# A one-core decoder step: how the memory tokens' squares are summed, where a spreading product stands, and when the second key tiles are scaled

## The chip, the core and the metric

The kernel runs on one core of a Trainium2 chip. A core has TensorE (PE in the profile, its weight loads apart as PEld), VectorE (DVE), ScalarE (ACT), GpSimd (POOL) and SyncE (SP, which issues most transfers here). Each engine works through its own queue in order and waits where an operand, written by another engine, is not there yet. The metric is device microseconds of one launch, taken as the median of several runs.

## What is computed

One decoder layer serves 1024 prompt tokens and 8 x 4 sample tokens with the same weights: a mixer of gated groups (A) and latent attention (B), a cross-attention into 256 memory tokens, and a gated feed-forward part with a short convolution. Two pieces of the reference matter here. The keys and values of the memory tokens:

```python
def mem_kv(mem, g_mem_in, w_mk, w_mv, g_mk):
    n, m, _ = mem.shape
    hm = rms_norm(mem, g_mem_in)
    k = rms_norm((hm @ w_mk).reshape(n, m, MEM_HEADS, MEM_HEAD_DIM), g_mk)
    v = (hm @ w_mv).reshape(n, m, MEM_HEADS, MEM_HEAD_DIM)
    return k, v
```

And the latent attention's queries and keys, each normalised per head before the scores (the prompt has 8 heads and blocks of 128 tokens; the samples attend to 4096 cached tokens):

```python
q = (rms_norm(cq, g_q_a) @ w_uq).reshape(n, t, MLA_HEADS, QK_HEAD)
q = qk_rope(rms_norm(q, g_qk_q), pos)
...
k = qk_rope(rms_norm(jnp.concatenate([k_nope, k_pe], axis=-1), g_qk_k), pos)
...
p = jax.nn.softmax(s, axis=-1)
```

`rms_norm(x, g)` is x divided by the root of its mean square, times g.

## The kernel before

Every larger product is taken in three: both operands are split into a high part (a cast, mostly on ScalarE) and a low part (the rest, mostly on VectorE, lines 200 to 207), and high x high, high x low and low x high are accumulated (`mm3`, line 185). The stages follow one another: input projection, prompt attention (`phase2a`), the samples' attention over the cache pages (`phase2b`), the memory tokens (`mem_kv`), the output projection, cross-attention, feed-forward.

**Order.** Inside a `manual_schedule` block the engines it names keep the order in which the program writes their instructions. All others are ordered by the framework's planner, which runs the program in simulated time when it is built. `behind(a, b)` adds an order without a wait: a stands behind b in the queue.

**The prompt attention** keeps TensorE, ScalarE, VectorE and GpSimd in written order; SP is the planner's. It runs in steps t = 0, 1, 2, ... Each step transposes probabilities (L996), starts the scores of the next unit (`units[n]["a"]`, products on L185, maxima on VectorE in L979 and L983), multiplies values (L1011), and then runs the functions in `extra[t]`: projections for later heads, the steps of their normalisation, transpositions of keys and queries (L949), and `weight_sums`, which prepare sums of feed-forward weights on GpSimd (L839 to L842) through two buffers that SP loads and stores. `times` lists the steps at which the 26 weight sums stand.

Heads 0 to 3 have two groups of four key and query tiles (`proj_group`). The second group's normalisation is a generator, `norm`, of which a call runs the part up to the next `yield`. Its parts are: the sums of squares and the start of the inverse root (L903 to L905, L232 to L234), two Newton steps (L241 to L246), the query's factors and rotation (L911), and the scaling of the keys (two VectorE products in L925, one GpSimd product in L926). Two parts run ahead of step 0; the rest of them, scaling included, at step 0. The transpositions that need these keys stand at step 2, and between the two, at step 1, stand the maxima of the next unit's third and fourth score tiles.

**The memory tokens** come at the end of the samples' attention, where only SP keeps the written order and the planner orders the other four engines. `mem_kv` is a generator as well, so that its parts are emitted between those of the last sample batch. It multiplies the keys of four heads (L1545), squares the raw memory rows for the mean square per token (L1558, summed on GpSimd in L1560 into `acc`), multiplies the values in four groups of twelve products (`values(0)`, `(2)`, `(4)`, `(6)`), sums the squares over partitions with one-column products against ones (L1579, L1581), takes the inverse roots, and scales the keys with diagonal products (L1600, L1601).

Beside it the last sample batch ends its softmax (`batch_softmax`): inverse roots of the last keys on GpSimd (L248 to L255), scaling of the scores (L1423), maxima (L1426, L1452), a transposition on TensorE (L1455), a maximum (L1458) made into a diagonal (L1460), and the spreading product, which brings the maxima to all partitions:

```python
self.spread = nc.tensor.matmul(bc, self.ones[:32], s["dg"], start=True, stop=True)
```

Then come a copy (L1465), a subtraction (L1466), the exponential (L1468) and the products with the cached values (L1475, L1477). The first product of `values(6)` is put `behind` the spreading product. The output projection (products of `mx0`, `mx1`, `mx2` with `w_o`) follows; its second and third thirds of tokens are loaded by SP as `raw<-mix` into a ring of three buffers, which the weights of `mem_kv` use as well.

Of the kernel before, what the change touches and what calls it, by code (L numbers as in the profile page):

```python
# [5 lines left out]
F32 = mybir.dt.float32  # L6
FR = mybir.dt.float32r
I32 = mybir.dt.int32
AF = mybir.ActivationFunctionType
ALU = mybir.AluOpType  # L10
AX = mybir.AxisListType
PSUM = bass.MemoryType.PSUM

P = 128
# [140 lines left out]
class Net:  # L155
# [502 lines left out]
    def phase2a(self):  # L658
# [31 lines left out]
        norm = qk1[9:]  # L690
# [52 lines left out]
        spread(late[1][1], 25, 30)  # L743
        spread(late[2][0], 24, 30)
        sums = [(i, z) for i in (NK, NK + 1, *range(NK)) for z in range(2)]
        times = (1, 2, 3, 4, 5, 7, 8, 9, 11, 12, 14, 15, 16, 25, 26, 27, 29, 30, 36, 37, 39, 40, 41, 43, 44, 46)
        for t, x in zip(times, sums):
            extra[t].append(lambda x=x: self.weight_sums(half(), *x))

# [17 lines left out]
        with tc.manual_schedule(engines={E.PE, E.Activation, E.DVE, E.Pool}):  # L767
            for f in preps[0][0], preps[0][1], v1[0], preps[1][0], preps[1][1]:
                f()
            for e in range(4):  # L770
                units[0]["a"](e)
                if e:
                    units[0]["e"](e - 1)
                    if e % 2:
                        v1[e // 2 + 1]()
            units[0]["e"](3)
            for f in norm[:2]:
                f()
            extra[0][:0] = norm[2:]
            extra[1][:0] = v1[3:]  # L780
            steps, outs, pend, V = [], {}, [], []
            self.lows = []
            t = 0
            for n, u in enumerate(units):
                for k, banks in enumerate(u["steps"]):
                    self.flush()
                    for b in banks:
                        u["T"](b)
                    for f in outs.pop(t, []):
                        f()  # L790
                    for f in pend:
                        f()
                    pend = []
                    for w, e in jobs[t]:
                        w["a"](e)
                        pend.append(lambda w=w, e=e: w["e"](e))
                    self.flush()
                    for f in V:
                        f()
                    V = [lambda u=u, b=b: u["V"](b) for b in banks]  # L800
                    if k == len(u["steps"]) - 1:
                        outs.setdefault(t + 2, []).append(u["copy"])
                        outs.setdefault(t + 3, []).append(u["out"])
                        if order[n] == (7, 0):
                            outs[t + 3].append(lambda: steps.append(mix()))
                    for f in extra[t]:
                        f()
                    t += 1
                    if t == 32:
                        steps.append(sample())  # L810
                    steps = [x for x in steps if next(x, 0) is None]
            self.flush()
            self.lows = None
            for fs in [V] + [outs[t] for t in sorted(outs)] + [[]] * 4:
                for f in fs:
                    f()
                steps = [x for x in steps if next(x, 0) is None]
            assert not steps
# [48 lines left out]
    def proj_group(self, p, pp, hf, i0, i1, s, c, tt=("tp", 4)):  # L867

        nc = self.nc
        m, tn = i1 - i0, TILES[i0][1]  # L870
        r = kk = q = None

        def alloc():
            nonlocal r, kk, q
            r = self.t(p, [P, 4, 2, 4], F32, "hr", 2)[:tn, :m]
            kk = self.t(p, [P, 4, 4, 96], F32, "k", 2) if i0 < 8 else None
            q = self.t(p, [P, 4, 4, 96], F32, "q", 2) if i0 < 8 else self.qs[:, hf * 4 : hf * 4 + 4].unsqueeze(1)

        def part(i, z):
            t0, e = TILES[i][0], i - i0  # L880
            a, b = (self.cqh, self.cql) if z == 0 else (self.ckh, self.ckl)
            x = [(a[:, k, t0 : t0 + tn], b[:, k, t0 : t0 + tn]) for k in range(2)]
            w, n = ((s["wq"], 384), (s["wk"], 256), (s["wv"], 256))[z]
            ps = self.t(pp, [P, 512], F32, *tt)[:tn, :n]
            self.mm3(ps, x, w)
            if z == 2:
                nc.scalar.copy(s["v"][:, i], ps.rearrange("p (h d) -> p h d", h=4))
                return
            pv = ps.rearrange("p (h d) -> p h d", h=4)
            if z == 0 or i < 8:  # L890
                nc.scalar.copy(kk[:, e, :, :64] if z else q[:, e], pv)
            sq = self.t(p, [P, 4, n // 4], F32, f"hsq{z}", 2)[:tn]
            if z == 1 and (i >= 4 if hf else i < 6):
                for j in range(4):
                    nc.scalar.activation(sq[:, j], pv[:, j], AF.Square, accum_out=r[:, e, z, j : j + 1])
                return
            nc.scalar.activation(sq, pv, AF.Square)
            nc.vector.tensor_reduce(r[:, e, z], sq, AX.X, ALU.add)

        def norm():  # L900
            sc = self.sq_tok[:tn, i0:i1].unsqueeze(2).broadcast_to([tn, m, 4])
            rq, rk = r[:, :, 0], r[:, :, 1]
            nc.vector.tensor_tensor(rq, rq, sc, ALU.mult)  # L903
            nc.vector.tensor_tensor(rq, rq, sc, ALU.mult)
            nc.vector.tensor_tensor(rk, rk, c["kss"][:tn, i0:i1].unsqueeze(2).broadcast_to([tn, m, 4]), ALU.add)  # L905
            rf = r.rearrange("p m z h -> p (m z h)")
            yield from self.rsqrt_steps(p, rf, rf, 1.0 / 96)
            yield
            if i0 < 8:

                nc.vector.tensor_tensor(c["rq"][:, i0:i1, hf * 4 : hf * 4 + 4], rq, sc, ALU.mult)  # L911
            else:
                nc.vector.tensor_tensor(rq, rq, sc, ALU.mult)
                nc.vector.tensor_tensor(q, q, rq.unsqueeze(3).broadcast_to([tn, m, 4, 96]), ALU.mult)
            for e in range(0, m, 2):
                z = slice(e, min(e + 2, m))
                x = q[:, z, :, 64:]
                self.rope_tok(p, x, x, [t[:tn, i0 + z.start : i0 + z.stop] for t in c["qt"]], 4, tn, z.stop - e)
            if i0 == 8:
                nc.vector.tensor_copy(self.rn[:, hf * 4 : hf * 4 + 4], rk[:, 0])  # L920
                return
            yield
            for a, eng in ((slice(0, m // 2), nc.vector), (slice(m // 2, m), nc.gpsimd if hf else nc.vector)):
                x = kk[:, a, :, :64]
                eng.tensor_tensor(x, x, rk[:, a].unsqueeze(3).broadcast_to([P, m // 2, 4, 64]), ALU.mult)  # L925
            nc.gpsimd.tensor_tensor(  # L926
                kk[:, :, :, 64:], self.kr[:, i0:i1].unsqueeze(2).broadcast_to([P, m, 4, 32]),
                rk.unsqueeze(3).broadcast_to([P, m, 4, 32]), ALU.mult,
            )
            for e in range(m):  # L930
                s["q", i0 + e], s["k", i0 + e] = q[:, e], kk[:, e]

        qk = [lambda i=i, z=z: part(i, z) for i in range(i0, i1) for z in range(2)]
        it = norm()
        return [alloc] + qk + [lambda: next(it, 0)] * 6, [lambda i=i: part(i, 2) for i in range(i0, i1) if i < 8]

    def head_prep(self, p, pp, h, s, c):

# [580 lines left out]
    def mem_kv(self, raws, wk0):  # L1519
# [5 lines left out]
        self.t(pp, [P, 512], F32, "free", 1)  # L1525
        st = self.t(pp, [P, 512], F32, "st", 1)
        mh, ml = (self.t(p, [P, 8, 256], FR, x) for x in ("mh", "ml"))
        acc = self.t(p, [P, 256], F32, "acc")
        mr = [r.rearrange("p (k n) -> p k n", k=4) for r in raws[1:3]]
        xs = [(mh[:, k], ml[:, k]) for k in range(8)]  # L1530
        kr, sq = [], []
# [1 line left out]
        for h in range(4):  # L1533
# [18 lines left out]
            sq.append(self.t(p, [P, 256], F32, "sq", 4))  # L1552
            nc.scalar.activation(sq[h], ps, AF.Square)
            yield
        for k in range(8):
            x = mr[k // 4][:, k % 4]
            s2 = acc if k == 0 else self.t(p, [P, 256], F32, "msq", 2)
            nc.scalar.activation(s2, x, AF.Square)  # L1558
            if k:
                nc.gpsimd.tensor_tensor(acc, acc, s2, ALU.add)  # L1560
        yield
        av = [self.t(pp, [P, 512], F32, f"v{i}") for i in range(2)]

        def values(k):
            wh, wl = (x.rearrange("p k n -> p (k n)").rearrange("p (k n) -> p k n", k=2) for x in self.stream(I["w_mv"][k // 2], 8))
            for i in range(2):
                t = slice(i * P, i * P + P)
                x = self.mm3(av[i], [tuple(x[:, t] for x in xs[k + e]) for e in range(2)],
                             [(wh[:, e], wl[:, e]) for e in range(2)], first=k == 0, last=k == 6)
                if k == 6 and i == 0:  # L1570
                    self.behind(x, self.spread)

        values(0)
# [4 lines left out]
            for i in range(2):  # L1578
                nc.tensor.matmul(st[:, 2 * h + i : 2 * h + i + 1], sq[h][:, i * P : i * P + P], self.ones[:, :1], start=True, stop=True)  # L1579
        for i in range(2):  # L1580
            nc.tensor.matmul(st[:, 8 + i : 9 + i], acc[:, i * P : i * P + P], self.ones[:, :1], start=True, stop=True)  # L1581
        rt = self.t(p, [P, 2], F32, "rt")
        r2 = self.t(p, [P, 2], F32, "r2")
        r = self.t(p, [P, 4, 2], F32, "r")
# [870 lines left out]
```

## Time and profile before

| what | value |
|---|---|
| median of 3 runs | 1844.83 us (1842.12 to 1846.34) |
| the profiled execution | 1843.82 us, its span 1842.1 us |
| mean granted clock of TensorE | 0.994 of full speed |
| TensorE busy | 1809.4 us, 98% of the span |
| VectorE, ScalarE, GpSimd busy | 1354.1, 922.9, 697.1 us |
| moved by the transfers | 261.18 MB, 142 GB/s on the mean |

A timeline's line reads: start in us from the beginning of the span, duration in us, engine, line of the kernel, operation, what it writes `<-` what it reads, shape, `x` the number of instructions merged, and in brackets how long the engine stood idle before it and for whom. A group's line reads: line, engine, operation, count, minimum/median/maximum duration in ns, first and last start. A stretch's line reads: its bounds, its length, each engine's busy time (PE, PEld, DVE, ACT, POOL, with counts), TensorE's granted clock, and the transfers' share and rate.

### The profile page before, as it was taken

The numbers are of one execution on the slowest core, as the hardware profiler recorded it, in microseconds if no ns is written. First come the engines' busy times: TensorE is split into PE (matmuls) and PEld (weight loads), VectorE is DVE, ScalarE is ACT, GpSimd is POOL, SyncE is SP. The second block draws the span as 40 slices with busy tenths as digits, with TensorE's granted clock in tenths as the row PEclk, the third lists the DMA queues.
The fourth block names the chain that finished last, engine by engine and source line by source line (L and its number), as shares of the span: only waits on it lengthen the run. The fifth ranks groups of instructions, "written<-read, shape, count | busy, mean of one in ns | idle before, by whom it ended". The sixth has DMA issues, their size and how long they took to land.

```text
span 1842.1 us, 39314 instructions
## 1 busy us (share of the span) xinstructions
PE 1809.4 (98%) x14222; PEld 1706.1 (93%) x14222; DVE 1354.1 (74%) x2805; ACT 922.9 (50%) x1916; POOL 697.1 (38%) x852
## 2 busy tenths in 40 slices
PE   9999999999999999999999999999999999999999
PEld 8999777779999999998899979999999999999999
DVE  7855767757778776786645666898888888878664
ACT  7435667766555555555433556533333333444442
POOL 1021555634444444453123110277766777400000
PEclk9999999999999999999999999999999999999999
DMA  8101353557767666654555155222222222495242
GB/s 324 42 25 66 109 194 109 183 167 210 222 191 194 193 176 188 181 168 145 160 161 181 62 179 169 98 82 70 93 82 70 70 82 75 140 328 173 78 154 77
DMA packets 153187, 261.18 MB, mean 142 GB/s; under 512 B 20897, under 2 KB 97538, under 8 KB 152994
## 3 DMA queue, kind: packets, MB, share of 16 engines
q1 hardware_dynamic: 152130, 257.63, 44.8%
q8 instruction: 112, 1.84, 0.4%
q10 hardware_dynamic: 864, 1.05, 0.2%
q14 instruction: 81, 0.66, 0.1%
HBM read 212.79 MB, written 45.82 MB: 140 GB/s over the span
## 4 chain that ended last, share of the span: by engine, by line
PE 73%; DVE 5%; issue 4%; ACT 2%; POOL 2%; DMA 1%; SPq 1%; DVEq 0%; POOLq 0%; ACTq 0%
PE s L185 16%; PE d L185 12%; PE b L185 8%; PE F L185 7%; PE E L185 7%; PE X L185 7%; PE A L185 3%; PE y L185 2%; PE o L1011 2%; PE tp L996 1%; PE tp L185 1%; PE o L1477 1%; PE tp L949 1%; PE t L185 1%; ACT pr L988 1%
## 5 line engine op out<-in xcount | busy, mean ns | idle before, releaser
L185 PE MATMUL s<-w2h,ch 128*128 128x288 f32 (+1 forms) x1024 | 304.4, 297 | 0.5 <-ACT S L1380 0.5
L185 PE MATMUL s<-w2h,cl 128*128 128x288 f32 (+1 forms) x1024 | 296.5, 290 | 3.3 <-POOL cl L1362 2.3
L185 PE MATMUL s<-w2l,ch 128*128 128x288 f32 (+1 forms) x1024 | 295.3, 288 | 0.0
L185 PEld LDWEIGHTS s<-w2h,ch 128*128 128x128 f32 x1024 | 193.3, 189 | 9.0 <-issue 2.5
L185 PEld LDWEIGHTS s<-w2h,cl 128*128 128x128 f32 x1024 | 193.1, 189 | 5.2 <-POOL cl L1362 3.9
L185 PEld LDWEIGHTS s<-w2l,ch 128*128 128x128 f32 x1024 | 193.5, 189 | 0.0
L1405 DVE TENSOR_REDUCE ss<-sq 128x16 f32<-128x1024 f32 x128 | 155.3, 1214 | 33.4 <-ACT sq L1402 33.0
L1362 POOL TENSOR_TENSOR cl<-cT,ch 128x512 fp32r<-128x512 f32 x64 | 83.8, 1310 | 126.7 <-ACT ch L1358 118.0
L1402 ACT ACTIVATE sq<-s 128x512 f32<-128x512 f32 x128 | 76.5, 598 | 89.5 <-PE s L185 89.5
L1399 ACT ACTIVATE sq<-s 128x512 f32<-128x512 f32 x128 | 76.7, 599 | 75.3 <-PE s L185 74.7
L200 ACT CAST a<-brb 128x528 fp32r<-128x528 f32 x77 | 48.8, 634 | 109.1 <-PE d L185 102.8
L185 PE MATMUL d<-a,w 128*128 128x264 f32 x768 | 95.2, 284 | 0.0
L185 PEld LDWEIGHTS d<-a,w 128*128 128x128 f32 x768 | 94.3, 188 | 0.0
L201 DVE TENSOR_TENSOR a<-brb,a 128x528 fp32r<-128x528 f32 x77 | 54.3, 707 | 53.7 <-ACT a L200 53.7
L2091 POOL TENSOR_TENSOR lo<-s,hi 128x1024 fp32r<-128x1024 f32 x20 | 63.8, 3190 | 45.7 <-ACT hi L2090 45.7
L185 PE MATMUL mm<-whi,xh 128*128 128x256 f32 (+3 forms) x272 | 77.2, 285 | 0.0
L185 PE MATMUL mm<-wlo,xh 128*128 128x256 f32 (+3 forms) x272 | 76.9, 285 | 0.1
L185 PE MATMUL mm<-whi,xl 128*128 128x256 f32 (+3 forms) x272 | 76.8, 286 | 0.0
L2146 ACT COPY a<-A 128x264 f32<-128x264 f32 x43 | 16.1, 374 | 118.4 <-PE A L185 114.4
L1358 ACT CAST ch<-cT 128x512 fp32r<-128x512 f32 x128 | 73.4, 626 | 2.1 <-DMA cT<-cT 2.1
L2212 POOL TENSOR_TENSOR cv<-cv,row 128x1056 f32<-128x1056 f32 x22 | 64.9, 2952 | 19.0 <-ACT cv L2211 19.0
L185 PE MATMUL d<-a,hi 128*128 128x264 f32 x552 | 72.0, 284 | 0.0
(746 smaller groups left out, 6350.3 us busy)
## 6 DMA issues: line engine op xcount, KB each, us to landing
cT<-cT SPq DMA_DIRECT2D x256, 160.0 KB, 2.7
ck<-ck SPq DMA_DIRECT2D x256, 144.0 KB, 3.3
raw<-w_up SPq DMA_DIRECT2D x44, 512.0 KB, 3.5
wsumd<-wsum SPq DMA_DIRECT2D x26, 512.0 KB, 3.6
actd<-cv SPq DMA_DIRECT2D x44, 264.0 KB, 2.3
brb<-actd SPq DMA_DIRECT2D x44, 264.0 KB, 5.7
wsum<-w_down SPq DMA_DIRECT2D x22, 512.0 KB, 3.4
raw<-wsumd SPq DMA_DIRECT2D x20, 512.0 KB, 3.6
```

Source lines behind the costliest of these rows:

```text
L185: x = self.nc.tensor.matmul(out, l, r, start=first and i == 0, stop=last and i == len(seq) - 1)
L200: first = {"act": nc.scalar.copy, "pool": nc.gpsimd.tensor_copy, "dve": nc.vector.tensor_copy}[eng](hi, src)
L201: low = lambda: nc.vector.tensor_tensor(lo, src, hi, ALU.subtract)
L949: nc.tensor.transpose(tp[:, j * P : j * P + P], s[x, g * 4 + j][:, h % 4], self.ident)
L1011: nc.tensor.matmul(u["o"][g : g + 64, o : o + m * P], s["v"][:, j, h % 4], th[:, z * P : (z + m) * P], start=j == 0, stop=b == len(banks) - 1,
L1358: nc.scalar.copy(d["h"][:, k], src[k])
L1362: (nc.vector if k else nc.gpsimd).tensor_tensor(d["l"][:, k], src[k], d["h"][:, k], ALU.subtract)
L1399: nc.scalar.activation(sq[:, 0], ps[:, :, n0 : n0 + 256], AF.Square)
L1402: nc.scalar.activation(sq[:, 1], pt.rearrange("p (e d) -> p e d", e=2), AF.Square)
L1405: yield lambda: nc.vector.tensor_reduce(s["ss"][:, g0 : g0 + 2].rearrange("p e (z h) -> p z e h", z=2), sq.rearrange("p z e (h d) -> p z e ...
L2091: eng.tensor_tensor(lo, src, hi, ALU.subtract)
L2212: nc.gpsimd.tensor_tensor(cv, cv, row, ALU.mult)
```

## The change

Three edits are made together.

1. In `mem_kv` the eight squares of 128x256 and the seven GpSimd sums are replaced by two squares of 128x1024, written over the raw memory rows, and two VectorE reductions, each of which adds four rows of 256 into a sum of its own. The sums over partitions take both, with two products per half of the tokens instead of one.
2. The first product of `values(4)`, not that of `values(6)`, is put behind the spreading product.
3. `norm` gets one more `yield`, ahead of its inverse root, so each group's normalisation has one more part. In the second group of heads 0 to 3, two Newton steps and the query's factors run at step 0, and the scaling of the keys goes to step 1, behind that step's two maxima. Of the weight sums the first five stand one step later: the list starts 2, 3, 4, 5, 6, 7 where it was 1, 2, 3, 4, 5, 7.

```diff
-        times = (1, 2, 3, 4, 5, 7, 8, 9, 11, 12, 14, 15, 16, 25, 26, 27, 29, 30, 36, 37, 39, 40, 41, 43, 44, 46)
+        times = (2, 3, 4, 5, 6, 7, 8, 9, 11, 12, 14, 15, 16, 25, 26, 27, 29, 30, 36, 37, 39, 40, 41, 43, 44, 46)
...
-            extra[0][:0] = norm[2:]
-            extra[1][:0] = v1[3:]
+            extra[0][:0] = norm[2:5]
+            extra[1][:0] = norm[5:] + v1[3:]
...
             rf = r.rearrange("p m z h -> p (m z h)")
+            yield
             yield from self.rsqrt_steps(p, rf, rf, 1.0 / 96)
...
-        return [alloc] + qk + [lambda: next(it, 0)] * 6, [lambda i=i: part(i, 2) for i in range(i0, i1) if i < 8]
+        return [alloc] + qk + [lambda: next(it, 0)] * 7, [lambda i=i: part(i, 2) for i in range(i0, i1) if i < 8]
...
-        acc = self.t(p, [P, 256], F32, "acc")
+        acc = [self.t(p, [P, 256], F32, f"acc{z}") for z in range(2)]
...
-        for k in range(8):
-            x = mr[k // 4][:, k % 4]
-            s2 = acc if k == 0 else self.t(p, [P, 256], F32, "msq", 2)
-            nc.scalar.activation(s2, x, AF.Square)
-            if k:
-                nc.gpsimd.tensor_tensor(acc, acc, s2, ALU.add)
+        for x, s2 in zip(mr, acc):
+            nc.scalar.activation(x, x, AF.Square)
+            nc.vector.tensor_reduce(s2, x.rearrange("p k n -> p n k"), AX.X, ALU.add)
...
-                if k == 6 and i == 0:
+                if k == 4 and i == 0:
                     self.behind(x, self.spread)
...
-            nc.tensor.matmul(st[:, 8 + i : 9 + i], acc[:, i * P : i * P + P], self.ones[:, :1], start=True, stop=True)
+            for z in range(2):
+                nc.tensor.matmul(st[:, 8 + i : 9 + i], acc[z][:, i * P : i * P + P], self.ones[:, :1], start=z == 0, stop=z == 1)
```

## The prediction

> **What bounds the kernel now.** First the page's busy times and the list of waits on TensorE, filtered to that engine (total us, times, longest).
>
> ```profile
> PE 1809.4 (98%) x14222; PEld 1706.1 (93%) x14222; DVE 1354.1 (74%) x2805; ACT 922.9 (50%) x1916; POOL 697.1 (38%) x852
> PE tp L996 <- ACT pr L988: 4.2, 8, 0.9
> PE s L185 <- DVE pr L983: 4.1, 6, 1.8
> PE o L1475 <- ACT S L1468: 2.3, 1, 2.3
> PE b L1600 <- DVE diag L1599: 1.0, 3, 0.6
> PE m L1455 <- DVE mx L1452: 0.8, 1, 0.8
> ```
>
> TensorE is busy 98% of the span, so an edit can win only a wait of TensorE or time at a lower clock. The change touches two places: the start of the prompt attention (about 207 to 215 us) and the memory tokens' keys and values (about 859 to 904 us). Busy time by stretch comes next (the number after the five engines is TensorE's granted clock).
>
> ```profile
> 214.00:216.00 2.00, 1.77 (x7) 1.28 (x8) 1.23 (x4) 0.31 (x1) 1.46 (x2) 0.75 0.48 165
> 216.00:218.00 2.00, 2.00 (x7) 1.79 (x7) 1.25 (x5) 0.00 (x0) 0.00 (x0) 0.50 0.51 152
> 884.00:886.00 2.00, 2.00 (x7) 1.70 (x7) 1.97 (x6) 0.00 (x0) 0.00 (x0) 0.51 0.67 236
> 886.00:888.00 2.00, 2.00 (x7) 1.53 (x6) 1.66 (x11) 0.00 (x0) 0.00 (x0) 0.64 0.80 234
> 894.00:896.00 2.00, 1.62 (x16) 1.51 (x20) 1.02 (x6) 1.01 (x2) 0.00 (x0) 0.57 0.21 78
> 896.00:898.00 2.00, 2.00 (x28) 1.86 (x24) 0.00 (x0) 1.98 (x4) 0.00 (x0) 0.58 0.35 131
> ```
>
> Behind each thin stretch the clock halves. At 884 us that lasts 4 x (0.49 + 0.36) = 3.4 us, at 894 us 4 x (0.43 + 0.42) = 3.4 us; where TensorE is the limit, each costs half of it, 1.7 us.
>
> Third, the timelines of the memory stretch, engine by engine: first GpSimd and ScalarE, then VectorE, then TensorE.
>
> ```profile
> L1560 POOL TENSOR_TENSOR acc<-acc,msq x7: 727/734/741, 871.6 to 879.9; 128x256 f32<-128x256 f32 x7
> 870.58 1.03 POOL L253 TENSOR_TENSOR rqh<-rqh,rqa 128x64 f32<-128x64 f32 x1
> 875.30 1.36 POOL L251 TENSOR_SCALAR rqa<-rqa 128x64 f32<-128x64 f32 x1
> 879.45 0.37 POOL L254 TENSOR_SCALAR rqh<-rqh 128x64 f32<-128x64 f32 x1
> 880.60 0.32 POOL L255 TENSOR_TENSOR ss<-rqh,rqy 128x64 f32<-128x64 f32 x1
> 872.34 0.42 ACT L1558 ACTIVATE msq<-ck 128x256 f32<-128x256 f32 x1 [2.54 <-POOL acc L1560]
> 867.78 3.65 DVE L201 TENSOR_TENSOR lo<-raw,hi 128x1024 fp32r<-128x1024 f32 x3
> 875.00 1.41 DVE L201 TENSOR_TENSOR lo<-raw,hi 128x1024 fp32r<-128x1024 f32 x1 [3.57 <-ACT hi L200]
> 880.95 0.43 DVE L1423 TENSOR_TENSOR S<-S,ss 128x256 f32<-128x256 f32 x1 [4.54 <-POOL ss L255]
> 885.67 0.22 DVE L1460 TENSOR_SCALAR dg<-ident,mm 32x32 f32<-32x32 f32 x1
> 881.45 1.17 PE L1579 MATMUL st<-ones,sq 128*128 128x1 f32 x10
> 883.43 0.27 PE L1455 MATMUL m<-ident,mx 128*32 128x128 f32 x1 [0.82 <-DVE mx L1452]
> 884.23 0.77 PE L185 MATMUL v<-hi,mh 128*128 128x512 f32 x1
> 890.06 0.40 PE L1463 MATMUL m<-dg,ones 32*128 32x32 f32 x2
> 894.38 0.64 PE L1475 MATMUL o<-cn,S 128*32 128x257 f32 x1 [2.31 <-ACT S L1468]
> 904.00 0.42 PE L185 MATMUL b<-mx0h,hi 128*128 128x384 f32 x1
> ```
>
> The last sample batch's softmax ends last here. Its inverse roots run on GpSimd until 880.92 with seven sums of the memory squares between their steps. VectorE stands 4.54 us for the result, TensorE 0.82 us for the maxima. The spreading product L1463 has its operand at 885.89 (885.67 + 0.22), but TensorE's queue has eighteen value products ahead of it and issues it at 890.06. Copy, subtraction and exponential follow, and TensorE stands 2.31 us before the first product with the probabilities.
>
> **Part 1: memory squares.** Eight ScalarE squares and seven GpSimd sums go; two squares of 128x1024 and two VectorE reductions come. Seven sums of 0.73 us are 5.1 us out of GpSimd's queue, and L251 (1.36 us against 0.37 for the like L254) ran beside the VectorE L201 of 875.00; earlier it can escape that. The nine root steps behind L253 (ends 871.61) take 0.32 to 0.37 us each undisturbed, 3.1 in all, so the roots end at about 874.7 instead of 880.92, 6.2 us earlier. ScalarE is off the path: it loses waits such as the 2.54 us. The squares, now in place, must wait for the low parts that VectorE takes from the same tile; what queues behind them on ScalarE are its casts of weights.
>
> The price is on VectorE. No row shows a reduction of four elements 256 apart; the nearest are these (minimum/median/maximum ns in the first):
>
> ```profile
> L1405 DVE TENSOR_REDUCE ss<-sq x128: 1202/1212/1223, 408.9 to 861.6; 128x16 f32<-128x1024 f32 x128
> 859.81 1.59 DVE L1426 TENSOR_REDUCE mx<-S 128x32 f32<-128x768 f32 x1 [0.42 <-POOL ck L1241]
> L1581 PE MATMUL st<-ones,acc x4: 250/250/353, 883.7 to 884.0; 128*128 128x1 f32 x4
> ```
>
> Along the line, 1024 elements cost 1.21 us; with a step, 768 cost 1.59, which makes 1024 x 1.59 / 768 = 2.12. I take the stepped row: 2 x 2.12 = 4.2 us (at least 2.4). [...]
>
> VectorE has 3.57 us idle ahead of 875.00 and 4.54 ahead of 880.95, so the reductions cost nothing on the path while they lie there. Without that cover they push L1423 and all behind it by up to 4.2 us. With both in front, L1423 starts about 871.4 + 4.2 = 875.6; from there to the operand took 4.9 us (880.95 to 885.89), so the operand comes at 880.5. The sums on TensorE go from two calls to four: L1581's four instructions begin at 883.7 and the value product behind them at 884.23, so some 0.55 us more.
>
> **Part 2: the spreading product.** It now stands ahead of the third group of value products (12) instead of the fourth. TensorE ends the second group at 881.45; the operand is there at 880.5, so I charge no wait. Eighteen value products took 884.23 to 890.06, 5.8 us, 4.1 without the clock's 1.7, which is 0.23 each. Between the spreading product and the probabilities' products now lie 24, 5.5 us, against the chain bc, subtraction, exponential, which took 890.06 to 894.38 = 4.3 us. So both the 0.82 and the 2.31 go. What is late next are the diagonals L1600, 1.0 us in the list of waits, which I leave. Of the two half-clock periods one should go with its 2.31 us; the other I keep, because the one-column sums (1.17 us for ten, above) still load TensorE thinly. Sum: -0.82 - 2.31 - 1.7 + 0.55 = -4.3 us. Bounds: both clock periods and the diagonals' wait gone gives -7.0; the spread late gives the rival below.
>
> [...]
>
> **Part 3: the second key tiles.** Timelines of 207 to 214 us, VectorE, GpSimd, ScalarE, TensorE, and the group of the scalings:
>
> ```profile
> 204.61 0.19 DVE L243 TENSOR_TENSOR rqa<-rqy 128x32 f32<-128x32 f32 x1
> 207.58 2.69 DVE L925 TENSOR_TENSOR k<-k,hr 128x512 f32<-128x512 f32 x2
> 210.19 0.55 DVE L979 CUSTOM_DVE_ANT_0 pr<-s,cmask 128x384 f32<-128x384 f32 x1
> L925 DVE TENSOR_TENSOR k<-k,hr x6: 677/951/1546, 189.8 to 300.8; 128x512 f32<-128x512 f32 x6
> 208.54 1.18 POOL L839 TENSOR_TENSOR wsum<-wsum 128x256 f32<-128x256 f32 x1
> 211.88 0.81 ACT L988 ACTIVATE pr<-pr,nm,rq 128x512 f32<-128x512 f32 x1
> 210.01 0.73 PE L949 MATMUL tp<-ident,k 128*96 128x128 f32 x4
> 212.84 0.33 PE L996 MATMUL tp<-ident,pr 128*128 128x128 f32 x1 [0.52 <-ACT pr L988]
> 213.89 0.41 PE L185 MATMUL s<-kTh,qTh 96*128 96x320 f32 x1 [0.73 <-ACT qTh L204]
> ```
>
> The two scalings (2.69 us) leave the place ahead of the maxima L979, but the root's first Newton step (four operations of 0.19 us like L243, 0.9 with their gaps) comes into it, since step one of the generator is cut in two. So the maxima start at 210.19 - 2.69 + 0.9 = 208.4, 1.8 us earlier, the exponentials end by 211.4 instead of 212.8, and the scalings start at 210.0. But TensorE reaches the transpositions of these keys at 210.01, as before: it now waits there. Alone the scalings take 0.68 each and end at 211.4; in their present company 2.69, ending at 212.7. The weight sums are moved one step back too (first five of 26), so GpSimd's queue has them right behind L926, beside the scalings again, and the two alternate as in the rows; I take 212.1. Then transposition, cast and scores start at about 213.6 instead of 213.9: -0.3 us, bounds -1.0 and +0.3. The half clock from 215 on stays, since as much idle time lies ahead of it. The weight sums end some 0.6 us later, and SP's loads and stores of their two buffers follow; nobody waits for them in this phase. The extra step also moves four projection products and root steps of later groups by one place. Each shift is under 1 us of work; I put it at 0, bounds -1.0 and +1.0, from the 4.1 us that TensorE waits for the maxima in all.
>
> **Sum.** -4.3 - 0.3 = -4.6 us on the profiled execution's 1843.82 (span 1842.1 and 1.7 around it) gives 1839.2. The median of the runs shown, 1844.83, lies 1.0 above that execution, so 1840.2.
>
> **Rivals.** (a) The stretch is held by something else: the out-projection's start at 904.00 needs the diagonals' chain on VectorE and weights and mixed rows from SP, which move only as buffers come free. Then what TensorE gains at 882 and 892 it gives back before 904, and only about 2 us stay: 1842.8. For it: L1600 waits already. Against it: roots and buffers come earlier with the same edits. (b) Slower: outside SP the planner orders this stretch by its own simulated times, and the spreading product now blocks the third value group. If VectorE's queue holds the 4.2 us of reductions between roots and diagonal, as late as the sums ended before, the operand comes at 885.9 + 4.2 = 890.1; TensorE, out of other work at 884.2, stands 5.9 us and wins back only the 2.31: 5.9 - 2.31 + 0.55 - 0.3 = +3.8, 1848.6. It decides from a wait of 2.31 - 0.55 + 0.3 = 2.1 us on, an operand behind 886.3. Against it: GpSimd is freed of 5.1 us first. (c) The waits go, the clock drops as often as before, because it drops for thin work such as the ten one-column sums of 881.45 and not for the waits: -0.82 - 2.31 + 0.55 - 0.3 = -2.9, 1841.9. For it: at 884 us it dropped behind a wait of only 0.82 us. Against it: at 894 us no such sums lay ahead. [...]
>
> **How the numbers follow.** A median of three that spreads over 4 us can tell about 0.2% (3.7 us) from no change. Forecast, all waits gone and one clock period: 0.52; (a) 0.15; (b) 0.15; (c) 0.18. Of the forecast's half some 0.44 lies beyond -3.7, by the bounds of parts 2 and 3, and 0.06 of (c); of (b) all but 0.01: faster 0.50, same 0.36, slower 0.14. The range goes from -9 (the lower bounds of parts 2 and 3, -7.0 - 1.0 - 1.0: 1835.8) to just short of rival (b), 1847.8.
>
> **What would show it.** Right: no GpSimd sums near 872 to 880, its roots done by 876, L1463's counterpart issued before 883, no wait of TensorE before the probabilities' products, and the first out-projection product at 899 to 900. Part 3 is right if the maxima start near 208.4 and TensorE waits at the keys' transpositions rather than the exponentials. Wrong if TensorE stands ahead of the spreading product, if the reductions pass 2.5 us each, or if the planner puts the roots' successors behind them.

## The result, and the profile after

The changed kernel takes 1832.8 us (median of five runs, 1830.28 to 1835.19) against 1844.83 (1842.12 to 1846.75): a ratio of 0.9937 with a 95% interval of 0.9920 to 0.9953. Two further sets, each beside its own runs of the kernel before, gave 0.9949 (0.9936 to 0.9963) and 0.9954 (0.9940 to 0.9967). Over all 17 runs the median is 1834.0; over 70 runs of the kernel before it is 1842.6. (One more run of the kernel before took 2169.5 us at a mean clock of 0.752 and is left out everywhere.) So it is 8.6 to 12 us faster, where 4.6 were forecast, and it lies 2 to 3 us below the range.

The page's busy times of after (that execution took 1831.31 us, its span 1829.6):

```profile
PE 1800.7 (98%) x14226; PEld 1698.6 (93%) x14226; DVE 1354.4 (74%) x2807; ACT 921.7 (50%) x1910; POOL 693.1 (38%) x845
```

The list of waits on TensorE (total us, times, longest):

```profile
PE s L185 <- DVE pr L984: 4.7, 7, 1.9
...
PE tp L997 <- ACT pr L989: 3.1, 6, 0.9
...
PE tp L950 <- DVE k L926: 1.5, 2, 0.8
...
PE b L1599 <- DVE diag L1598: 1.0, 3, 0.6
```

The 2.3 us before the probabilities' products and the 0.8 us for the maxima are gone. The diagonals' 1.0 us stands as before. New are 1.5 us before the transpositions of the second key tiles (L950). Busy time by stretch:

```profile
210.00:212.00 2.00, 0.61 (x3) 0.17 (x2) 1.97 (x5) 1.37 (x4) 1.84 (x3) 1.00 0.00 0
212.00:214.00 2.00, 1.54 (x11) 1.31 (x12) 0.87 (x3) 1.47 (x3) 1.92 (x3) 1.00 0.03 8
214.00:216.00 2.00, 1.61 (x8) 1.09 (x8) 1.35 (x4) 0.17 (x1) 1.76 (x4) 1.00 0.77 262
216.00:218.00 2.00, 2.00 (x9) 1.21 (x9) 1.78 (x9) 0.00 (x0) 0.52 (x1) 1.00 0.06 10
884.00:886.00 2.00, 2.00 (x22) 1.16 (x24) 1.86 (x7) 1.27 (x2) 0.00 (x0) 1.00 0.01 2
886.00:888.00 2.00, 2.00 (x44) 1.21 (x40) 1.66 (x11) 0.27 (x1) 0.00 (x0) 1.00 0.84 231
```

The column after the five engines is TensorE's granted clock. It is 1.00 in all of these rows, where before had 0.50 and 0.51 at 216 and 884 us. Now the timelines of the memory stretch, GpSimd first, then ScalarE, VectorE and TensorE:

```profile
869.78 1.05 POOL L255 TENSOR_TENSOR ss<-rqh,rqy 128x64 f32<-128x64 f32 x1
861.37 2.02 ACT L1557 ACTIVATE ck<-ck 128x1024 f32<-128x1024 f32 x2
865.55 3.94 DVE L1558 TENSOR_REDUCE acc<-ck 128x256 f32<-128x1024 f32 x2
870.86 0.43 DVE L1424 TENSOR_TENSOR S<-S,ss 128x256 f32<-128x256 f32 x1 [0.21 <-POOL ss L255]
874.60 0.23 DVE L1461 TENSOR_SCALAR dg<-ident,mm 32x32 f32<-32x32 f32 x1
857.24 0.36 PE L1546 MATMUL b<-mh,wk0h 128*128 128x256 f32 x1 [0.82 <-ACT mh L204]
877.64 0.40 PE L1464 MATMUL m<-dg,ones 32*128 32x32 f32 x2
878.44 1.03 PE L1580 MATMUL st<-ones,acc 128*128 128x1 f32 x8
885.12 0.40 PE L1476 MATMUL o<-cn,S 128*32 128x257 f32 x1
893.12 0.42 PE L185 MATMUL b<-mx0h,hi 128*128 128x384 f32 x1
1600.61 11.87 PE L185 MATMUL d<-a,w 128*128 128x264 f32 x96
```

The roots end on GpSimd at 870.83, VectorE stands 0.21 us for them instead of 4.54, the reductions take 1.97 us each, and in this profile no wait is left ahead of the spreading product or the probabilities. Two rows of before complete the landmarks:

```profile
861.86 0.36 PE L1545 MATMUL b<-mh,wk0h 128*128 128x256 f32 x1 [0.82 <-ACT mh L204]
1613.11 11.87 PE L185 MATMUL d<-a,w 128*128 128x264 f32 x96
```

The span fell by 12.5 us (1842.1 to 1829.6). Of that 4.6 lies ahead of the first memory product (861.86 to 857.24; other profiles of the same kernels have it at 859.66, and at 858.65 and 858.68, so it varies by 1 to 2 us from run to run); 6.3 between it and the first out-projection product (42.14 us before, 35.88 after); and 1.6 between there and the down projection (709.11 before, 707.49 after), where nothing was edited.

### The profile page after: what moved, and what is told of

Same layout as the page of the kernel before. It is cut to its first block, busy times and chain, and to the rows that moved or that the text cites. A ratio compares the mean times of both kernels' runs of the same rounds, so it can differ in the third digit from the quotient of the medians.

```text
span 1829.6 us, 39308 instructions
## 1 busy us (share of the span) xinstructions
PE 1800.7 (98%) x14226; PEld 1698.6 (93%) x14226; DVE 1354.4 (74%) x2807; ACT 921.7 (50%) x1910; POOL 693.1 (38%) x845
## 4 chain that ended last, share of the span: by engine, by line
PE 70%; issue 5%; SPq 5%; DVE 3%; DMA 2%; ACT 2%; POOL 1%; DVEq 0%; POOLq 0%; ACTq 0%
PE s L185 12%; PE d L185 12%; PE b L185 8%; PE F L185 7%; PE X L185 7%; PE E L185 7%; PE A L185 3%; PE y L185 3%; SPq L1335 2%; SPq L1331 2%; PE o L1012 2%; PE tp L997 1%; PE tp L185 1%; SPq L1310 1%; PE o L1478 1%
```

## The experiments

All runs are beside runs of the kernel before on the same chip, whose medians were 1842.3, 1842.3, 1843.2 and 1843.0 in the four sets. A gain in us goes by the ratio; the medians can put it 1 to 2 us higher or lower. "Clock" is the mean granted clock over a kernel's runs; the kernel before has 0.9948 over 70 runs, the changed one 0.9984 over 17.

**Each edit alone.** First the kernel before itself.

> The kernel before, unchanged, for the granted clock of each of its runs. Theory A (the clock halves because TensorE idles too much at the waits that the change takes away): every run shows a clock of about 0.994 to 0.996 and 1842 to 1847 us. [...]

1841.8 us, ratio 0.9996 (0.9987 to 1.0005), each run's clock from 0.994 to 0.996: theory A's numbers.

Edit 1 alone, the squares and sums:

```
...
-            nc.scalar.activation(s2, x, AF.Square)
-            if k:
-                nc.gpsimd.tensor_tensor(acc, acc, s2, ALU.add)
+        for x, s2 in zip(mr, acc):
+            nc.scalar.activation(x, x, AF.Square)
+            nc.vector.tensor_reduce(s2, x.rearrange("p k n -> p n k"), AX.X, ALU.add)
```

> Edit 1 alone (two squares in place, two VectorE reductions). Theory A: all of the memory stretch's gain (6.3 us between the two profiles) and the 1.6 us behind 904 us come with it, -8 us, 1837; the spreading product stands ahead of the third value group without edit 2. Rival: the spreading product needs edit 2, so that TensorE still waits for the exponential or the clock still drops: -3 to -5, 1840 to 1842.

1835.64 us, ratio 0.9961 (0.9947 to 0.9974): 7.2 us, clock 0.9960, near theory A's 8. In its order TensorE already issues the spreading product ahead of all 24 value products of the last two groups.

Edit 2 alone, `k == 6` to `k == 4` in the line that holds the value products behind the spreading product:

> Edit 2 alone (spreading product ahead of the third value group). The roots still end at about 881, so the operand comes at 885.9 and TensorE waits 1.7 us ahead of it from 884.2; the 2.3 us before the probabilities go. Theory A: -0.6 us of waits, a clock period more or less on top, 1842.5 to 1846 (no change). Rival: it carries the memory stretch's gain, -4 or more, under 1841.

1843.4 us, ratio 1.0007 (0.9998 to 1.0016): nothing, as theory A said. In its trace the wait before the probabilities' products falls from 2.31 to 0.72 us, but the diagonals' wait grows from 1.0 to 1.8, and TensorE still takes 38.8 us at full clock from the first memory product to the first out-projection product. Edits 1 and 2 together give, on every engine's queue, the order that edit 1 alone gives. Edit 2 is worth nothing here, with or without edit 1.

Edit 3 alone, the key tiles:

```
...
+            yield
             yield from self.rsqrt_steps(p, rf, rf, 1.0 / 96)
...
-            extra[0][:0] = norm[2:]
-            extra[1][:0] = v1[3:]
+            extra[0][:0] = norm[2:5]
+            extra[1][:0] = norm[5:] + v1[3:]
...
-        times = (1, 2, 3, 4, 5, 7, 8, ...
+        times = (2, 3, 4, 5, 6, 7, 8, ...
...
```

> Edit 3 alone (one more part in the normalisation, scalings behind two maxima, weight sums one step later). Theory A: -4.6 us, 1840, with no half clock between 214 and 240 us. Theory B: only the waits' difference of under 1 us, 1844, and the half clock is there in some runs and not in others. My prediction's step for it was -0.3.

1839.12 us, ratio 0.9985 (0.9976 to 0.9994): 2.8 us, clock 0.9974. That lies between the theories: less than 4.6, and its profile still has a half-clock stretch at 217 us. Edits 1 and 3 alone add up to 10.0 us and 0.0038 of clock (0.0012 and 0.0026); the changed kernel shows 8.6 to 12 us and 0.0036.

**Is it the place of the spreading product?** Edit 1, with the spreading product held back until 13 of the 24 value products are issued:

```
-                if k == 6 and i == 0:
-                    self.behind(x, self.spread)
+                if k == 6:
+                    self.behind(*((x, self.spread) if i == 0 else (self.spread, x)))
```

> Edit 1 alone (squares in place, sums on VectorE), with the spreading product held behind the first 13 of the 24 value products, near its place in the kernel before; the feed-forward's order is that of edit 1. Theory A (edit 1 gains because the planner brings the spreading product forward): spreading product 3.0 us later than in edit 1 (13 x 0.23), a wait of about 1.8 us before the probabilities' products is back and a clock period with it: 1.8 to 3.5 us above edit 1's 1835.6, 1837.4 to 1839.1. Theory B (the freed GpSimd queue suffices): the same as edit 1 within 0.7.

1835.8 us, ratio 0.9963 (0.9950 to 0.9977): the same as edit 1. Timeline of this kernel, VectorE, then TensorE:

```profile
877.48 0.23 DVE L1460 TENSOR_SCALAR dg<-ident,mm 32x32 f32<-32x32 f32 x1
886.55 0.40 PE L1463 MATMUL m<-dg,ones 32*128 32x32 f32 x2
890.75 0.71 PE L1598 MATMUL b<-diag,ones 128*128 128x128 f32 x4 [1.04 <-DVE diag L1597]
891.39 0.40 PE L1475 MATMUL o<-cn,S 128*32 128x257 f32 x1
```

The operand lies ready from 877.71, the product goes at 886.55, and still no wait of 2.31 us comes back: eleven value products and the first diagonals cover the chain, and the diagonals' one wait takes its place. What counts is that the operand is early.

**Do the reductions cost anything?** The kernel before with `acc` taken from a single square of 128x256, no sum at all:

> The kernel before without the sum of the memory squares: one square of a 128x256 slice stands for all eight, so neither GpSimd's seven sums nor VectorE's two reductions run. The planner's order of TensorE is that of edit 1, spreading product and feed-forward included. Theory A (edit 1 gains only by taking the sums off GpSimd's queue; its reductions on VectorE are hidden): within 0.7 us of edit 1's 1835.6. Theory B (the reductions still cost on the path): 1.5 to 4 us less than edit 1, 1831.6 to 1834.1.

1834.79 us, ratio 0.9960 (0.9947 to 0.9974). The median lies 0.8 us below edit 1's, but it was taken beside other runs of the kernel before; the ratios, 0.9960 and 0.9961, are the same. In the profiles the way from the first memory product to the first out-projection product takes 37.42 us, and 37.45 with edit 1, with one half-clock stretch in each. So the two reductions cost nothing that these runs can show.

**The clock: fill the waits.** The kernel before with extra products into tiles that TensorE fills next:

```
+                if (h, G, b) == (1, 0, 0) and z in (1, 3):
+                    for _ in range(3):
+                        nc.tensor.matmul(tp[:, z * P : z * P + P], s["qT", 1, 0][0][:, :P], s["kT", 1][0][:, :P], start=True, stop=True)
...
+                if (h, G, e, z) == (0, 1, 0, 0):
+                    for _ in range(3):
+                        nc.tensor.matmul(sv, s["qT", 1, 0][0][:, :P], s["kT", 1][0][:, :w], start=True, stop=True)
```

> The kernel before, with nine extra products at the head of the prompt scores, written into the tiles that TensorE fills next, where it stands for the exponentials and the cast of the keys (about 1.6 us of work in 2.0 us of waits); the scalings stay where they were. Theory A (the waits made the clock halve): the scores start as before within 0.3 us, the half-clock stretch behind 214 us goes in most runs, mean clock 0.9948 to about 0.997, time 2 us less (1 to 3.4) than before's 1842.3. Theory B (edit 3 gained by bringing the key transpositions earlier): clock 0.995 and the same time, or 0.3 us more.

1841.64 us, ratio 0.9988 (0.9977 to 1.0000), clock 0.9965 but spread from 0.995 to 0.999. Theory A in part: the scores start as before (10.42 us behind the sums of squares on L903 in both kernels), and the clock rises, but in a third of the runs only (four of twelve have 0.998 or 0.999 and take 1836 to 1838 us, the others 1839 to 1845; none of the 70 runs of the kernel before is above 0.996). Busy time of this kernel:

```profile
210.00:212.00 2.00, 2.00 (x18) 1.47 (x16) 1.96 (x5) 0.72 (x3) 1.84 (x3) 1.00 0.03 8
212.00:214.00 2.00, 1.46 (x11) 1.17 (x10) 0.52 (x4) 1.95 (x6) 1.84 (x4) 1.00 0.00 0
214.00:216.00 2.00, 1.48 (x7) 0.96 (x6) 1.50 (x3) 0.96 (x2) 1.84 (x3) 0.92 0.78 262
216.00:218.00 2.00, 2.00 (x7) 1.75 (x7) 1.35 (x6) 0.00 (x0) 0.23 (x1) 0.50 0.23 50
```

Here TensorE is busier from 210 to 216 us than in the changed kernel (4.94 of 6 us against 3.76), yet its clock halves at 216 and the other's doesn't. Nor does the order decide it: k1 and b1 below have the same instructions here and 4.62 and 4.63 busy us of the 6, and the clock halves at 216 us in the profile of k1 and not in that of b1. The busy share alone does not set it.

The same, and three products into the last batch's accumulator:

```
...
+                    x = nc.tensor.matmul(s["o"][:32], self.ones[:, :32], self.cn[:, :257], start=True, stop=True)
+                    self.behind(x, self.spread)
```

> The same, and three extra products into the value accumulator of the last sample batch, behind the spreading product, where TensorE stands 2.31 us ahead of the probabilities' products. The planner gives this kernel another order near 1169 us, in which the 1.8 us wait for the feed-forward's roots is gone as it is with edit 1. Theory A: the half clock behind 892 us goes too: the first filler's 2.0, one period of 1.7 and the 1.7 of the feed-forward, 5.4 us less than before: 1836.9 (1835.5 to 1838.5), mean clock about 0.998. Theory B (only waits count, not the clock): 1.7 less from the feed-forward alone, 1840.6.

1836.14 us, ratio 0.9957 (0.9943 to 0.9971), clock 0.9977. The total is theory A's, but not cleanly: in the new order ScalarE takes the exponential ahead of other work, so part of the wait went by order and not by filling, and its profile has a half-clock stretch at 900 us in place of the one at 894.

**The clock: the thin sums.** In the changed kernel TensorE doesn't wait near 880 us at all, and yet the clock halves there in one of its three profiles. Of that profile (the second set), TensorE's timeline and the busy times by stretch:

```profile
878.19 0.95 PE L1577 MATMUL st<-ones,sq 128*128 128x1 f32 x8
879.40 0.61 PE L1577 MATMUL st<-ones,sq 128*128 128x1 f32 x4
879.87 1.41 PE L1580 MATMUL st<-ones,acc 128*128 128x1 f32 x8
```

```profile
878.00:880.00 2.00, 2.00 (x18) 1.90 (x16) 0.49 (x1) 1.23 (x2) 0.00 (x0) 1.00 0.69 224
880.00:882.00 2.00, 2.00 (x11) 1.90 (x11) 1.97 (x3) 0.01 (x1) 0.00 (x0) 0.59 0.61 172
882.00:884.00 2.00, 2.00 (x6) 1.52 (x6) 1.65 (x11) 1.08 (x1) 0.00 (x0) 0.50 0.59 182
```

Ahead lie twenty instructions of one column (the twelve products of the sums are 24 instructions in the records; four stand earlier). Of six profiles with edit 1, these thin sums and no wait just ahead of them, three have a half clock in or right behind them. Two kernels give them 32 columns (the squares' sums likewise):

```
...
-  nc.tensor.matmul(st[:, 8 + i : 9 + i], acc[z][:, i * P : i * P + P], self.ones[:, :1], start=z == 0, stop=z == 1)
+  nc.tensor.matmul(sx[:, 8 + i], acc[z][:, i * P : i * P + P], self.ones[:, :32], start=z == 0, stop=z == 1)
```

First on the changed kernel:

> The changed kernel with the twelve one-column sums' products over 32 columns of ones instead of one (16 instructions, the same order, the same weights loaded). Theory A (the clock halves near 880 us because these products are thin, not because TensorE waits: it does not wait there): no half clock between 876 and 892 us in the profile, mean clock 0.9995 against 0.9985, time 0.5 to 1.7 us less than the changed kernel's 1833.6. Theory B (chance, or another cause): the clock there still halves in some runs, mean 0.998 to 0.999, time the same or 0.3 us more.

1833.23 us, ratio 0.9951 (0.9937 to 0.9965), clock 0.9986: no half clock from 876 to 892 us in its profile, but the mean clock and the time are theory B's. Undecided by itself.

**Why is edit 3 alone worth only 2.8?** Its move of the scalings, without the extra step and with the weight sums in their places, and then the rest without the move:

```
-            extra[0][:0] = norm[2:]
-            extra[1][:0] = v1[3:]
+            extra[0][:0] = norm[2:4]
+            extra[1][:0] = norm[4:] + v1[3:]
```

This is k1; k2 has the `yield`, the seven steps and the new `times` of edit 3, and the two `extra` lines as before.

> Of edit 3 only the move of the key scalings behind the two maxima; the generator keeps its six steps, the weight sums their places. Theory A (the move itself gains): the wait before the scores of about 234 us falls from 1.8 to about 0.9 us, clock near 0.997, time near edit 3's 1839.1 (1838.3 to 1840.0). Theory B (the extra step, which shifts the later groups' work by one place, gains): wait 1.8 us, clock 0.995, 1842.3.

1837.18 us, ratio 0.9970 (0.9958 to 0.9982): 5.5 us, clock 0.9973.

> The rest of edit 3 without that move: the generator's extra step and the weight sums one step later, the key scalings still ahead of the two maxima. Theory A: as before, 1842.3 with a clock of 0.995. Theory B: 1839.1 with 0.997, and the wait of about 234 us at 0.9 us.

1842.14 us, ratio 0.9997 (0.9988 to 1.0006), clock 0.9947. So the move gains and the rest does not. The shifted places of the weight sums alone change no queue's order; the extra step is what tells edit 3 from k1.

The traces tell the two apart to 0.01 us. The first line is the start of the second group's sums of squares on VectorE in the kernel before, where the first score product behind these key tiles stands at 213.89 us. Then come the same two lines of the changed kernel, of k1, of edit 3 alone and of k2:

```profile
203.47 0.16 DVE L903 TENSOR_TENSOR hr<-hr,sq_tok 128x16 f32<-128x16 f32 x1
203.61 0.17 DVE L903 TENSOR_TENSOR hr<-hr,sq_tok 128x16 f32<-128x16 f32 x1
213.75 0.42 PE L185 MATMUL s<-kTh,qTh 96*128 96x320 f32 x1 [0.39 <-ACT qTh L204]
204.15 0.16 DVE L903 TENSOR_TENSOR hr<-hr,sq_tok 128x16 f32<-128x16 f32 x1
213.39 0.41 PE L185 MATMUL s<-kTh,qTh 96*128 96x320 f32 x1 [0.38 <-ACT qTh L204]
203.69 0.17 DVE L903 TENSOR_TENSOR hr<-hr,sq_tok 128x16 f32<-128x16 f32 x1
213.84 0.41 PE L185 MATMUL s<-kTh,qTh 96*128 96x320 f32 x1 [0.38 <-ACT qTh L204]
203.80 0.16 DVE L903 TENSOR_TENSOR hr<-hr,sq_tok 128x16 f32<-128x16 f32 x1
215.12 0.48 PE L185 MATMUL s<-kTh,qTh 96*128 96x320 f32 x1 [0.72 <-ACT qTh L204]
```

The distance is 10.42 us before, 10.14 in the changed kernel, 9.24 in k1, 10.15 with edit 3 and 11.32 in k2. So the move brings the scores 1.18 us forward and the extra step puts them 0.9 back, each with or without the other: the step lays one more Newton step ahead of the maxima or the scalings. k2 has the feed-forward's better order as well (1.8 us, below), which the 0.9 half undoes.

One gain of the move was not in the prediction's sum. Around 232 us in a run of the kernel before (VectorE, GpSimd, TensorE), and then in k1:

```profile
232.72 0.44 DVE L903 TENSOR_TENSOR hr<-hr,sq_tok 32x4 f32<-32x4 f32 x1
233.28 0.71 DVE L905 TENSOR_TENSOR hr<-hr,kss 32x4 f32<-32x4 f32 x1
234.21 0.58 DVE L233 TENSOR_SCALAR rqy<-rqx 32x8 int32<-32x8 int32 x1
231.62 0.73 POOL L839 TENSOR_TENSOR wsum<-wsum 128x256 f32<-128x256 f32 x1 [3.77 <-DMA wsum<-w_down]
235.91 0.47 PE L185 MATMUL s<-kTh,qTh 96*128 96x448 f32 x1 [1.70 <-DVE pr L983]
```

```profile
231.14 0.14 DVE L903 TENSOR_TENSOR hr<-hr,sq_tok 32x4 f32<-32x4 f32 x1
231.39 0.14 DVE L905 TENSOR_TENSOR hr<-hr,kss 32x4 f32<-32x4 f32 x1
231.77 0.16 DVE L233 TENSOR_SCALAR rqy<-rqx 32x8 int32<-32x8 int32 x1
232.09 0.73 POOL L839 TENSOR_TENSOR wsum<-wsum 128x256 f32<-128x256 f32 x1 [3.64 <-DMA wsum<-w_down]
233.04 0.47 PE L185 MATMUL s<-kTh,qTh 96*128 96x448 f32 x1 [0.41 <-DVE pr L983]
```

GpSimd's next weight sums start when their load lands, near 232 us in both. VectorE's little root operations come before them in k1 and among them in before, where three of them take 1.73 us instead of 0.44. The difference, 1.29, is just what TensorE's wait loses (1.70 to 0.41). Over all profiles this wait is 1.5 to 1.9 us in the nine with the scalings in their old place, 0.86 with edit 3 alone and 0.41 in the other seven with them moved, whether the clock had halved at 217 us or not.

**A version that takes the best of both.** b1 is edit 1 and k1, without edit 2 and the rest of edit 3; b2 is b1 with the wide sums; the changed kernel ran beside them.

> Edit 1 and, of edit 3, only the move of the scalings (k1): the generator keeps six steps, and edit 2 is left out, as it adds nothing to the order that edit 1 gives. Theory A (the extra step is what makes edit 3 worth less than its move alone): edit 1's 7.2 and the move's 5.5 less the 1.8 us of the feed-forward's order, which both contain: 10.9 us less than before, some 1831.5, and 2 us less than the changed kernel. Theory B (edit 3 and the move alone differ by the planner's order of the feed-forward only): the changed kernel's time within 1 us, 1833 to 1834.5.

1832.59 us (1831.59 to 1833.02), ratio 0.9942 (0.9930 to 0.9954), clock 0.9982: 10.7 us, near theory A's 10.9.

> The changed kernel once more, on the chip of the two others of this call: 1833.6 with a mean clock of 0.9985 by the eleven runs so far, and no half clock between 212 and 228 us in the profile (neither of its two profiles nor that of the wide sums had one there, eight of eight with the scalings in their old place had).

1833.84 us (1832.17 to 1838.38), clock 0.9982; this profile does have a half clock at 217 to 224 us, so that expectation missed. An earlier set of the same kernel, expected as follows:

> The changed kernel itself, beside the kernels of this call. Theory A (idle time of TensorE at the removed waits is what made the clock halve): the granted clock stays at 0.998 or more as a mean over the runs, time 1832 to 1834 us. Theory B (the clock of the first runs was a lucky phase): a mean clock of about 0.996, time 1836 to 1838.

1834.46 us, clock 0.9982: above the first five runs (0.9990), below theory B.

> The same as b1 with the twelve sums' products over 32 columns. Theory A (thin products make the clock halve near 880 us): mean clock 0.001 above b1's and 1 to 1.7 us less. Theory B (they do not): b1's clock and time within 0.7 us.

1831.05 us (1829.38 to 1831.8), ratio 0.9933 (0.9921 to 0.9945), clock 0.9993. Against b1, 0.0011 of clock and 1.5 us, theory A's numbers; and all its runs lie below all six of the changed kernel beside it. So b2 is the fastest version found. That the wide sums are the reason is not shown: neither of the two profiles has a half clock near 880 us, both take 35.9 us from the first memory product to the first out-projection product, and their 1.1 us of difference lies ahead of the first, where the two kernels are the same. Whether b1 beats the changed kernel stays open: 1.2 us, and the intervals overlap; in the traces its scores start 0.9 us earlier, by the step that it leaves out.

## Why the prediction came out as it did

**What held.** GpSimd's roots do end early (870.83; 874.7 was worked out, on a stretch that began 4.6 us later than it now does, so 870.1 by the same sum). The stepped reduction was sized from the 128x768 row at 2.12 us and takes 1.97; that no cover is missing is shown by the kernel without sums. The stepped reduction is the dearer one, 1.97 us (3.94 for the two) against 1.21 along the line, though it also writes 256 sums instead of 16, which no run separates. TensorE's 0.82 and 2.31 us go, the diagonals' 1.0 stays. At full clock the memory stretch is 38.7 us before (42.14 less half of 6.8 us at half clock) and 35.9 after: 2.9, where the waits less the extra sums made 2.6. In part 3 the maxima start at 208.6 (208.4 said), TensorE waits at the key transpositions as said, and the scores start 0.28 us earlier (0.3 said), counted from the first sum of squares on L903 (10.14 us behind it instead of 10.42). The 0.9 us that it gave to the extra Newton step is what k1 and k2 show. Rivals (a) and (b) did not come: TensorE kept what it gained at 882 and 892 up to 904, and nothing stood ahead of the spreading product.

**What failed, step by step.**

1. "The other I keep": of the two half-clock periods of the memory stretch I took one away. The first profile lost both, 1.7 us more than the sum, and so did the third. In the second, two periods (6.9 us at half clock between 880 and 888) stand together behind the one-column sums, where the prediction had placed the one that it kept.
2. "The half clock from 215 on stays, since as much idle time lies ahead of it." It goes in most runs. Of nine profiles with the scalings in their old place nine have a half clock near 216 us; of eight with them moved, three. The reason I gave was incomplete as well: idle time bears on it (filling the waits raised the clock in a third of the runs) but doesn't decide it alone. The clock is the largest single part of the miss. 0.9948 to 0.9984 is 13 us less at half clock in 1840 (2 x 0.0036 x 1840), worth at most 6.6 us. Within the runs of one kernel, 0.001 of clock goes with 1.3 us (before, 70 runs) and 1.5 us (after, 17), so 0.0036 is some 5 us. My sum had 1.7 for it.
3. I put the shift of the later groups' work at 0: the collision near 232 us, 1.3 us, was visible in before's own trace and was not looked for.
4. The feed-forward was not in the sum. Between 904 and 1613 us nothing was edited, but the planner orders it anew whenever its simulated times move. In before, in the kernels of edit 2 and of edit 3 and in the filled one, the first row products stand behind their roots; with edit 1, k1 or k2 others come ahead of them, and from the first out-projection product to the down projection TensorE takes 707.3 to 707.5 us instead of 709.1. The same line in a run of the kernel before and in the changed one:

```profile
1168.07 1.48 PE L2044 MATMUL A<-ident,hr 128*128 128x128 f32 x10 [1.82 <-DVE hr L246]
```

```profile
1163.64 1.37 PE L2043 MATMUL A<-ident,hr 128*128 128x128 f32 x10
```

That is 1.6 to 1.8 us of luck, not of the edit's mechanism. That k1 got it and edit 3 did not, together with the 0.9 us that the extra step costs edit 3, makes up their difference of 2.7; their clocks are the same (0.9973 and 0.9974).

5. Part 2's reason. The waits went because of part 1: moving the spreading product (edit 2) is worth nothing, and holding it back costs nothing.

Put together: 2.9 of waits in the memory stretch, 0.3 of part 3, 1.3 at 232 us and 1.6 of the feed-forward make 6.1 without the clock, where my sum had 2.9; with some 5 of clock it is 11. The 17 runs show 8.6, the first five 12.0. The clock's share is the loosest term, an estimate from the slopes, so the sum does not close better than to 2 or 3 us.

**The half clock's length.** In the seventeen profiles each half-clock stretch ahead of 1820 us lasts about 3.4, 6.8 or 10.2 us (an estimate from the granted clock of every 4 us, summed as in the prediction), and the same kernel has them in some executions only: the changed kernel has one at 216 us in its third profile and not in its first two. Near 880 us the clock halves in one profile with no idle time of TensorE in the records at all (busy for all 10.00 us from 878 to 888), behind one-column products. Rival (c), in which the clock drops as often as before, 1841.9, did not come: the time is 8 us below it.

**Still open.** What quantity sets the half clock. Waits bear on it, thin products may, and chance does from run to run; a kernel with 3.8 of 6 us busy kept its clock and one with 4.9 of 6 lost it.

## What to carry to other kernels

When one engine is 98% busy, look at its granted clock over many runs before costing waits: here a change forecast to win 3 us of waits came with a clock worth some 5 more, and a single profile could not tell. Moving work off a queue that others wait for was what gained (edit 1 alone, 7.2 us); writing the order by hand was worth nothing: with the earlier operand the planner had already drawn it, and without that operand the wait only moved to the diagonals. And a planner's reordering of an untouched stretch can be as large as an edit (1.6 to 1.8 us here): measure each edit alone and read the landmarks of every stretch.

## What the runs showed of the hardware

- In the changed kernel's second profile a half-clock stretch cost TensorE time where nothing waited: behind twenty one-column products the 128x512 product's spacing went from 0.23 to 0.43 us. Widening them to 32 columns cost nothing (eight took 1.06 us against 1.03), and went with 0.0011 more clock in one pair of kernels and 0.0002 in the other, which does not show that it is the cause.
- The clock differed where the instructions didn't: k1 and b1 have the same ones from 210 to 216 us, 4.62 and 4.63 us busy, and then a granted clock of 0.53 and of 1.00 from 216 to 218.
- VectorE operations on 32x4 elements, 0.14 us in k1 with GpSimd idle, took 0.44 and 0.71 in a run of the kernel before while GpSimd's 128x256 sums (0.73 us each) ran.
- ScalarE squared the two tiles of 128x1024 in place in 2.02 us.
